# An encoder layer's routing stage: where the low one-hots are made, where the first expert rows stand, and how early the gate's weights are split

## The chip, the cores and the metric

The kernel runs on one core of a Trainium2 chip. The metric is the device time of one execution in microseconds; three runs of the kernel before are shown, and their median counts. The engines are TensorE (PE, with its weight loads PEld), VectorE (DVE), ScalarE (ACT), GpSimd (POOL) and SyncE (SP). SyncE issues most transfers, GpSimd the gathers, ScalarE some stores.

## What is computed

One encoder layer on 512 tokens of width 1024 in float32: attention, a layer norm, then a feed-forward part that picks experts per token (PEER), plus a gated embedding, and a second layer norm. The change touches the part behind the attention:

```python
q = (xb @ w_q).reshape(PEER_CHUNK, PEER_HEADS, PEER_KEY_DIM)
s1 = jnp.einsum('thd,kd->thk', q[..., :half], sub_keys[0])
s2 = jnp.einsum('thd,kd->thk', q[..., half:], sub_keys[1])
v1, i1 = lax.top_k(s1, PEER_TOPK)
v2, i2 = lax.top_k(s2, PEER_TOPK)
...
idx = (e1 * PEER_N_KEYS + e2).reshape(PEER_CHUNK, PEER_HEADS * PEER_TOPK)
g = jax.nn.softmax(cv.astype(jnp.float32), axis=-1).reshape(PEER_CHUNK, -1).astype(xb.dtype)
u = u_table[idx]
hpre = jnp.einsum('td,ted->te', xb, u)
act = g * jax.nn.gelu(hpre, approximate=False)
return jnp.einsum('te,ted->td', act, v_table[idx])
...
gate = jax.nn.sigmoid(h @ ple_gate_w[i] + ple_gate_b[i])
h = layer_norm(DN_ALPHA * h + ffn + ple, ln2_g[i], ln2_b[i])
```

## The kernel before

The 512 tokens are four chunks of 128. Every token has 128 picks among 16384 experts. Three ways of using the expert tables stand side by side. For chunk 0 the picked rows of both tables are gathered, one row per token at a time (128x1024, 512 KB). Chunk 1, called own in the code, gathers its rows of the first table (`rows`, L960 to L968: a gather by GpSimd, then a multiply and sum on VectorE) and uses the second table densely. Chunks 2 and 3 use both tables densely: TensorE multiplies all 128 blocks of 128 experts with the tokens, and a dense matrix of weights, mostly zero, picks out what counts.

**The dense weights** are made by `build_g` (L885), once each for chunks 2, 3 and 1, in 16 steps of eight tokens (OT). A step makes one-hots `oh` of the two halves of each expert's number on VectorE (L934), multiplies the first half's one-hots with the weight, once with its high part in 16 bits and once with the rest (`ow_hi`, `ow_lo`, L945, both on VectorE), and has TensorE multiply the one-hots (32 matmuls of 128x128, L912, `products`). ScalarE copies the sums out (`g_st`, L923, `leave`) and every second step sends 1 MB to DRAM (L926).

**Splits.** TensorE's operands in 32 bits are split into a high and a low part, and three matmuls (`mm3`, L111 to L113) make one product. ScalarE makes the high part, VectorE the rest. The gate's weights go through `gate_cut` (L1054): `g_hi` on ScalarE, `g_lo` on VectorE (L1059).

**The order of the work** is the order in which the code issues it, on all engines. Two parts run interleaved. The main line works on VectorE: the last searches of the query projection (a loop over g of 2 to 16, one projection of 24 matmuls a step, and the search for the 16 best keys on VectorE), `route` for the half of chunk 1, the searches that were put off (`later`), `route` and `build_g` for chunks 2 and 3, the searches and `route` of chunk 0, and the last `build_g`. Behind each piece, `run` (L1138) lays in work of the second line, `pe_work` (`gate_and_leads`, L1094), for as many microseconds as the piece yielded, times PACE; AHEAD is a lead of 14. That line has eight blocks of the first table (FIRST; eight matmuls a block, L1030, tiles `raw` or, for the first EARLY of them, `early`), then 16 steps of the gate with a block behind each (three behind a half), then blocks up to 104 (LEAD). `run` also lays in rows of chunk 1, `own`, by a share of the same amounts (OWN, OWN_SOON, OWN_G). In the projection loop `own` gets a fixed amount per step (OWN_B: 3.6 in steps 9 to 11, 2.3 from 12 on) and one more row behind the search from step 12 on. A row there has the tile `row` with two buffers; later the names `whi`, `wlo`, `row` take turns, six buffers in all.

Small pieces of the second line (the split of the gate's next weights, and `gate_end`, which adds the bias, applies tanh on ScalarE and multiplies with the tile `pl`, L1071 to L1082) wait in a list `tasks`, of which one is issued at every second matmul of a block. A load on SyncE's queue that must wait holds all loads that were issued behind it.

## Time and profile before

| | us |
|---|---|
| median of three runs | 1570.45 (1569.98 to 1571.4) |
| the profiled execution, its own time | 1569.65 |
| its span, first to last instruction | 1567.9 |
| TensorE busy | 1473.4 |
| VectorE busy | 1280.0 |
| ScalarE busy | 542.1 |
| GpSimd busy | 613.4 |

The engine columns are busy time within the span. A row of the time line has the start, the duration, the engine, the line of the kernel, the operation, the tiles written and read, and in brackets how long the engine had stood idle and what ended that. PEclk is the part of TensorE's full clock that was granted. One float32 matmul of a block shows as two records. The mean rate of the transfers over the span is 291 GB/s; between 573.8 and 782.5 us it is 392 to 397 GB/s.

### The profile page before, as it was taken

Reading aid. Unit: us, or ns where it says so; the run is one execution under the profiler, and the core shown is the slowest. Engines: PE = TensorE matmul, PEld = TensorE weight load, DVE = VectorE, ACT = ScalarE, POOL = GpSimd, SP = SyncE. Lnnn points to the kernel's source line nnn. Section 1 sums busy time; section 2 is a strip of 40 time slices with the busy share of each in tenths; the row PEclk is TensorE's granted clock in tenths of the full one; section 3 lists DMA queues with packets and bytes.
Section 4 is the critical chain, followed back from the end, with each engine's and each line's share of the span. In section 5 each row is a group of like instructions: output and inputs, shape, how many; then the busy total and the mean of one; then the engine's idle time right before and its main releaser. Section 6 shows DMA issues by size and latency. Waiting matters only on the chain.

```text
span 1567.9 us, 21888 instructions
## 1 busy us (share of the span) xinstructions
PE 1473.4 (94%) x7715; PEld 1231.0 (79%) x7715; DVE 1280.0 (82%) x2636; ACT 542.1 (35%) x915; POOL 613.4 (39%) x534
## 2 busy tenths in 40 slices
PE   6999999999878999989999889999899999999996
PEld 4788777788767877777787778888788888888885
DVE  7366795657679999899998967988788998899998
ACT  3265784433211132212322223443333333333332
POOL 1013110043443344445205526667434456545650
PEclk9999999999989999999999999999999999999998
DMA  7233340334678899999979999999999999999992
GB/s 231 64 112 92 89 128 28 93 126 136 227 252 278 311 337 374 418 403 397 384 228 364 415 405 379 403 398 392 381 398 392 367 398 385 392 392 391 368 327 91
DMA packets 189856, 460.36 MB, mean 294 GB/s; under 512 B 16561, under 2 KB 80433, under 8 KB 186673
## 3 DMA queue, kind: packets, MB, share of 16 engines
q1 hardware_dynamic: 121552, 213.55, 38.4%
q0 software_dynamic: 58400, 208.69, 35.6%
q10 hardware_dynamic: 9792, 36.70, 5.8%
q8 instruction: 61, 1.00, 0.3%
q14 instruction: 51, 0.41, 0.1%
HBM read 415.11 MB, written 40.89 MB: 291 GB/s over the span
## 4 chain that ended last, share of the span: by engine, by line
PE 56%; DVE 15%; issue 11%; POOL 8%; DMA 8%; ACT 1%; POOLq 0%; SPq 0%; DVEq 0%; ACTq 0%
PE acc L111 10%; PE acc L113 10%; PE acc L112 10%; DMA row<-in_u_rows_dram,s_ix 4%; PE pj L111 3%; PE pj L112 3%; PE pj L113 3%; POOL row L965 3%; POOL wlo L965 3%; POOL whi L965 3%; PE mm L111 2%; PE mm L113 2%; PE mm L112 2%; DMA raw<-in_uT_dram 1%; PE hp L1030 1%
## 5 line engine op out<-in xcount | busy, mean ns | idle before, releaser
L1030 PE MATMUL mm<-whole,raw 128*128 128x256 f32 x1168 | 270.0, 387 | 8.6 <-DMA raw<-in_uT_dram 8.6
L1295 POOL DMA_INDIRECT gat<-in_v_rows_dram,i_sel x128 | 191.4, 1495 | 167.0 <-DVE base L1297 134.9
L1030 PEld LDWEIGHTS mm<-whole,raw 128*128 128x128 f32 x1168 | 221.3, 193 | 41.1 <-DMA raw<-in_uT_dram 5.6
L111 PE MATMUL acc<-v_hi,a_hi 128*128 128x512 f32 x456 | 179.1, 393 | 4.0 <-ACT v_hi L96 4.0
L112 PE MATMUL acc<-v_lo,a_hi 128*128 128x512 f32 x456 | 178.8, 392 | 0.5 <-DVE v_lo L97 0.5
L113 PE MATMUL acc<-v_hi,a_lo 128*128 128x512 f32 x456 | 178.4, 391 | 0.1
L1280 POOL DMA_INDIRECT gat<-in_u_rows_dram,i_sel x89 | 134.0, 1505 | 110.4 <-DVE gat L1286 75.6
L1297 DVE SCALAR_TENSOR_TENSOR base<-gat,hdot,base 128x1024 f32<-128x1024 f32 x128 | 165.1, 1290 | 1.6
L97 DVE TENSOR_TENSOR wlo<-raw,whi 128x1024 fp32r<-128x1024 f32 (+4 forms) x103 | 118.8, 1153 | 47.4 <-ACT whi L96 45.3
L96 ACT CAST v_hi<-v_raw 128x1024 fp32r<-128x1024 f32 x76 | 79.8, 1053 | 180.5 <-issue 101.5
L96 ACT CAST whi<-raw 128x1024 fp32r<-128x1024 f32 (+4 forms) x103 | 102.5, 995 | 90.6 <-PE pj L112 22.2
L111 PE MATMUL acc<-whi,a_hi 128*128 128x512 f32 x312 | 123.0, 396 | 0.7 <-ACT whi L96 0.7
L113 PE MATMUL acc<-whi,a_lo 128*128 128x512 f32 x312 | 123.4, 396 | 0.0
L112 PE MATMUL acc<-wlo,a_hi 128*128 128x512 f32 x312 | 123.3, 396 | 0.0
L97 DVE TENSOR_TENSOR v_lo<-v_raw,v_hi 128x1024 fp32r<-128x1024 f32 x76 | 92.5, 1218 | 22.0 <-ACT v_hi L96 22.0
L1286 DVE SCALAR_TENSOR_TENSOR gat<-gat,h 128x1024 f32<-128x1024 f32 x89 | 105.0, 1220 | 0.0
L111 PEld LDWEIGHTS acc<-v_hi,a_hi 128*128 128x128 f32 x456 | 86.1, 189 | 22.5 <-ACT v_hi L96 4.4
L113 PEld LDWEIGHTS acc<-v_hi,a_lo 128*128 128x128 f32 x456 | 86.0, 189 | 19.2 <-DVE a_lo L97 0.6
L112 PEld LDWEIGHTS acc<-v_lo,a_hi 128*128 128x128 f32 x456 | 86.2, 189 | 18.5 <-DVE v_lo L97 1.0
L965 POOL DMA_INDIRECT row<-in_u_rows_dram,s_ix x52 | 63.0, 1212 | 83.5 <-DVE row L967 53.4
L967 DVE SCALAR_TENSOR_TENSOR row<-row,h_s 128x1024 f32<-128x1024 f32 x52 | 67.6, 1301 | 26.8 <-DMA row<-in_u_rows_dram,s_ix 26.8
L1030 PE MATMUL hp<-whole,raw 128*128 128x256 f32 x368 | 84.6, 385 | 0.4 <-ACT ge L1014 0.4
(394 smaller groups left out, 3328.9 us busy)
## 6 DMA issues: line engine op xcount, KB each, us to landing
raw<-in_uT_dram SPq DMA_DIRECT2D x120, 512.0 KB
v_raw<-in_v_rows_dram SPq DMA_DIRECT2D x78, 512.0 KB
raw<-in_v_rows_dram SPq DMA_DIRECT2D x50, 512.0 KB
g_dram<-g_st ACTq DMA_DIRECT2D x24, 1024.0 KB
ge_dram<-ge ACTq DMA_DIRECT2D x44, 256.0 KB
g_wide<-g_dram SPq DMA_DIRECT2D x9, 1024.0 KB
raw<-in_w_in_dram SPq DMA_DIRECT2D x17, 512.0 KB
raw<-in_w_q_dram SPq DMA_DIRECT2D x16, 512.0 KB
```

Source lines behind the costliest of these rows:

```text
L96: nc.scalar.copy(hi, src)
L97: nc.vector.tensor_tensor(lo, src, r32(hi), op=OP.subtract)
L111: nc.tensor.matmul(ps, a[0], b[0], start=start, stop=False)
L112: nc.tensor.matmul(ps, a[0], b[1], start=False, stop=False)
L113: nc.tensor.matmul(ps, a[1], b[0], start=False, stop=stop)
L965: nc.gpsimd.indirect_dma_start(out=u[:], out_offset=None, in_=u_rows, in_offset=bass.IndirectOffsetOnAxis(ap=ix[:, k:k + 1], axis=0))
L967: nc.vector.scalar_tensor_tensor(u, u, 1.0, x, op0=OP.mult, op1=OP.mult, accum_out=dots[:, k:k + 1])
L1030: nc.tensor.matmul(ps[:, :N_U], raw[:, k], whole[:, k, :], start=(k == 0), stop=(k == 7))
L1280: nc.gpsimd.indirect_dma_start(out=u[:], out_offset=None, in_=u_rows, in_offset=bass.IndirectOffsetOnAxis(ap=i_sel[:, c, k:k + 1], axis=0))
L1286: nc.vector.scalar_tensor_tensor(u, u, 1.0, h[c], op0=OP.mult, op1=OP.mult, accum_out=hdot[:, c, k:k + 1])
L1295: nc.gpsimd.indirect_dma_start(out=u[:], out_offset=None, in_=v_rows, in_offset=bass.IndirectOffsetOnAxis(ap=i_sel[:, c, k:k + 1], axis=0))
L1297: nc.vector.scalar_tensor_tensor(base[c], u, hdot[:, c, k:k + 1], base[c], op0=OP.mult, op1=OP.add)
```

## The change

It has three parts, and numbers that go with them.

The low one-hots: `w_lo` stays in 32 bits, one value per token and pick, and `ow_lo` is made by ScalarE, eight multiplies of 128x128 a step with the weight as a scale from the tile, instead of one VectorE instruction of 128x1024. They stand behind the copies of the sums of the step before. The yields of a step go from 2.45 to 1.8 in all.

The rows in the projection: one row before the search and one behind it, from step 12 on, instead of two and one; the row (or piece of routing) behind the search begins at step 10.

The gate's weights: `g_hi` and `g_lo` have two buffers, and the weights of step j+2 are split behind step j's matmuls, where those of step j+1 were. `pl` has three buffers instead of four and EARLY is 6 instead of 7. PACE is 1.06, OWN_G 1.5.

```diff
-PACE = 1.0
+PACE = 1.06
-EARLY = 7
+EARLY = 6
-OWN_B = (3.6, 2.3)
+OWN_B = (3.6, 1.1)
-OWN_G = 1.15
+OWN_G = 1.5
...
-        wx = [bt.tile([128, 128, 2], F16, name=n) for n in ("w_hi", "w_lo")]
-        w_ps = ps[:, 256:384].unsqueeze(2).to_broadcast([128, 128, 2])
+        w_hi = bt.tile([128, 128, 2], F16, name="w_hi")
+        w_lo = bt.tile([128, 128], F32, name="w_lo")
...
             yield 1.15
-            ow = []
-            for n, x in zip(("ow_hi", "ow_lo"), wx):
-                y = bt.tile([128, OT, 128], F16, name=n)
-                nc.vector.tensor_tensor(y.rearrange("p t (a b) -> p t a b", b=2),
-                                        oh[:, 0].rearrange("p t (a b) -> p t a b", b=2),
-                                        x[:, t0:t0 + OT].unsqueeze(2).to_broadcast([128, OT, 64, 2]), op=OP.mult)
-                ow.append(y)
-                if n == "ow_hi":
-                    yield 0.65
+            ow = [bt.tile([128, OT, 128], F16, name=n) for n in ("ow_hi", "ow_lo")]
+            nc.vector.tensor_tensor(ow[0].rearrange("p t (a b) -> p t a b", b=2),
+                                    oh[:, 0].rearrange("p t (a b) -> p t a b", b=2),
+                                    w_hi[:, t0:t0 + OT].unsqueeze(2).to_broadcast([128, OT, 64, 2]), op=OP.mult)
             if ahead:
                 leave(ahead[0], sums)
+            for t in range(OT):
+                nc.scalar.mul(ow[1][:, t], oh[:, 0, t], w_lo[:, t0 + t:t0 + t + 1])
...
-        hi = rw.tile([128, 512], F32R, name="g_hi")
-        lo = rw.tile([128, 512], F32R, name="g_lo")
+        hi = rw.tile([128, 512], F32R, name="g_hi", bufs=2)
+        lo = rw.tile([128, 512], F32R, name="g_lo", bufs=2)
...
-            pl[c] = rg.tile([128, 512], F32, name="pl", bufs=4)
+            pl[c] = rg.tile([128, 512], F32, name="pl", bufs=3)
...
+        def cut_next():
+            w, cut = gate_cut(graw.pop(0))
+            ws.append(w)
+            return [cut[0], nothing, cut[1]]
+
         for n in range(FIRST):
-            if n == FIRST - 2:
-                w, cut = gate_cut(graw.pop(0))
-                tasks.extend([cut[0], nothing, cut[1]])
+            if n >= FIRST - 2:
+                tasks.extend(cut_next())
             yield from lead_block()
+        graw += [gate_raw(2), gate_raw(3)]
...
-            if j + 1 < 16:
-                w, cut = gate_cut(graw.pop(0))
-                if j + 2 < 16:
-                    graw.append(gate_raw(j + 2))
-                tasks[0:0] = [cut[0], nothing, cut[1]]
+            if j + 2 < 16:
+                tasks[0:0] = cut_next()
+                if j + 4 < 16:
+                    graw.append(gate_raw(j + 4))
...
-            if g > 11:
+            if g > 9:
                 next(own)
```

Three places show how the order of the instructions changes. The first is VectorE in the projection loop, steps 13 and 14; `row` is a gathered row of chunk 1, `sc` the scores that are searched. Before:

```order
L692 MAX_INDEX i_all<-v_all,tk_t 128x8
L967 SCALAR_TENSOR_TENSOR row,s_dot<-row,h_s 128x1024 x3
L684 MAX v_all<-sc 128x8
L686 MAX_INDEX i_all<-v_all,sc 128x8
L688 MATCH_REPLACE tk_t<-v_all,sc 128x128
L690 MAX v_all<-tk_t 128x8
```

And now:

```order
L692 MAX_INDEX i_all<-v_all,tk_t 128x8
L964 SCALAR_TENSOR_TENSOR row,s_dot<-row,h_s 128x1024 x2
L684 MAX v_all<-sc 128x8
L686 MAX_INDEX i_all<-v_all,sc 128x8
L688 MATCH_REPLACE tk_t<-v_all,sc 128x128
L690 MAX v_all<-tk_t 128x8
```

Between two searches there are two rows where there were three: the one behind the first search and one before the second.

The second place is ScalarE in the first build; `g_st` are the sums that are copied out, `ge` a block's result, `ge_dram` and `g_dram` are stores. Before:

```order
L923 ACTIVATE g_st<-tr 128x128x4 x2
L926 DMA g_dram<-g_st 128x2048
L1014 ACTIVATE ge<-mm 128x256
L923 ACTIVATE g_st<-tr 128x128x4 x2
L1014 ACTIVATE ge<-mm 128x256
L1016 DMA ge_dram<-ge 128x512
```

And now:

```order
L923 ACTIVATE g_st<-tr 128x128x4 x2
L926 DMA g_dram<-g_st 128x2048
L949 ACTIVATE ow_lo<-oh,w_lo 128x128 x8
L923 ACTIVATE g_st<-tr 128x128x4 x2
L949 ACTIVATE ow_lo<-oh,w_lo 128x128 x8
L1011 ACTIVATE ge<-mm 128x256
L923 ACTIVATE g_st<-tr 128x128x4 x2
```

Behind every pair of copies stand the eight multiplies of the next step, and they come before the following block's result.

The third place is SyncE's queue at the end of the gate's first half, with the semaphores that each load waits for; `pl` is what the gate is multiplied with, `raw` a block of the first table, `g_raw` the gate's weights. Before:

```order
L1071 DMA pl<-ple_dram 128x512 [waits DMAHW7_49]
L1071 DMA pl<-ple_dram 128x512 [waits DMAHW0_49]
L1071 DMA pl<-ple_dram 128x512
L1071 DMA pl<-ple_dram 128x512 [waits DMAHW2_49]
L1007 DMA raw<-in_uT_dram 128x1024 [waits DMAHW3_49,PE_49]
```

And now:

```order
L1048 DMA g_raw<-in_gate_w_dram 128x512 [waits DMAHW3_49,DMAHW0_49,DVE_49]
L1068 DMA pl<-ple_dram 128x512
L1068 DMA pl<-ple_dram 128x512 [waits DMAHW2_49]
L1068 DMA pl<-ple_dram 128x512
L1068 DMA pl<-ple_dram 128x512 [waits DMAHW5_49,DMAHW1_49,DVE_49]
L1004 DMA raw<-in_uT_dram 128x1024 [waits DMAHW6_49,PE_49]
```

The fourth load of `pl` now waits for VectorE, and the loads of `raw` stand behind it.

More of the change, by code (lines that the diff above doesn't have):

```diff
@@ L898, in build_g @@
                            .unsqueeze(3).to_broadcast([128, nq, OT, 2]))
-        wx = [bt.tile([128, 128, 2], F16, name=n) for n in ("w_hi", "w_lo")]
-        w_ps = ps[:, 256:384].unsqueeze(2).to_broadcast([128, 128, 2])
+        w_hi = bt.tile([128, 128, 2], F16, name="w_hi")
+        w_lo = bt.tile([128, 128], F32, name="w_lo")
         scale = W_OWN if c == NGC else W_MAX
-        nc.scalar.mul(wx[0], w_ps, scale)
-        nc.vector.scalar_tensor_tensor(wx[1], w_ps, scale, wx[0], op0=OP.mult, op1=OP.subtract)
+        nc.scalar.mul(w_hi, ps[:, 256:384].unsqueeze(2).to_broadcast([128, 128, 2]), scale)
+        nc.vector.scalar_tensor_tensor(w_lo, ps[:, 256:384], scale, w_hi[:, :, 0], op0=OP.mult, op1=OP.subtract)
         yield 0.5
@@ L1096, in gate_and_leads @@
         graw = [gate_raw(0), gate_raw(1)]
+        ws = []
+        def cut_next():
+            w, cut = gate_cut(graw.pop(0))
+            ws.append(w)
+            return [cut[0], nothing, cut[1]]
         for n in range(FIRST):
-            if n == FIRST - 2:
-                w, cut = gate_cut(graw.pop(0))
-                tasks.extend([cut[0], nothing, cut[1]])
+            if n >= FIRST - 2:
+                tasks.extend(cut_next())
             yield from lead_block()
+        graw += [gate_raw(2), gate_raw(3)]
         for j in range(16):
@@ L1107, in gate_and_leads @@
             k = j % 8
+            w = ws.pop(0)
             for c in range(4):
```

## The prediction

> **What bounds the kernel now.** I read the page first, for which engine is full, then the waits of TensorE, then the time line at those waits, and last a table by stage.
>
> ```profile
> PE 1473.4 (94%) x7715; PEld 1231.0 (79%) x7715; DVE 1280.0 (82%) x2636; ACT 542.1 (35%) x915; POOL 613.4 (39%) x534
> PE   6999999999878999989999889999899999999996
> ```
>
> TensorE is busy for 94% of the span, and the change leaves its work alone. So a gain can only come out of the 94.5 us in which it is idle and out of its slow clock. The slices put most of the idle time between 400 and 960 us: the end of the query projection, the gate and the routing. All edits lie there. After that TensorE is full, and a gain made before is kept.
>
> The waits of TensorE from 380 to 500 us, the column being total, times and longest, and the time line of TensorE there:
>
> ```profile
> PE mm L112 <- DVE g_lo L1059: 14.2, 2, 10.2
> PE mm L113 <- POOL wlo L768: 5.2, 2, 2.8
> 400.00:420.00 20.00, 14.81 (x65) 11.67 (x65) 14.29 (x27) 3.50 (x10) 9.46 (x7) 0.91 0.63 197
> 402.39 0.40 PE L111 MATMUL mm<-hTh,whi 128*128 128x512 f32 x1
> 402.63 0.40 PE L112 MATMUL mm<-hTl,whi 128*128 128x512 f32 x1
> 425.87 1.05 PE L727 MATMUL tr<-skT,q_t 128*128 128x128 f32 x8
> 426.76 20.94 PE L1030 MATMUL hp<-whole,early 128*128 128x256 f32 x96
> 450.80 0.58 PE L111 MATMUL mm<-g_hi,hTh 128*128 128x512 f32 x1
> 461.56 0.80 PE L112 MATMUL mm<-g_lo,hTh 128*128 128x512 f32 x1 [10.18 <-DVE g_lo L1059]
> 462.15 0.63 PE L113 MATMUL mm<-g_hi,hTl 128*128 128x512 f32 x1
> 462.58 0.63 PE L111 MATMUL mm<-g_hi,hTh 128*128 128x512 f32 x1
> 474.37 0.80 PE L112 MATMUL mm<-g_lo,hTh 128*128 128x512 f32 x1 [4.07 <-DVE g_lo L1059]
> ```
>
> TensorE stands for 5.2 us in the projection and for 14.2 us at the first two gate steps. Behind the gate waits the clock is low: the matmuls start 0.43 us apart (462.15 to 462.58) where they started 0.24 us apart before (402.39 to 402.63). Why the split of the gate's weights came so late, the time line of VectorE shows:
>
> ```profile
> 414.28 3.08 DVE L967 SCALAR_TENSOR_TENSOR row<-row,h_s 128x1024 f32<-128x1024 f32 x1 [1.59 <-DMA row<-in_u_rows_dram,s_ix]
> 445.10 0.29 DVE L684 MAX8 v_all<-sc 128x8 f32<-128x128 f32 x1
> 460.82 0.69 DVE L1059 TENSOR_TENSOR g_lo<-g_raw,g_hi 128x512 fp32r<-128x512 f32 x1
> ```
>
> TensorE computed the scores of the last but one projection at 425.87, and VectorE began the last search at 445.10, some 19 us behind. Each step gives VectorE three rows of 512 KB with two buffers to gather into, so it waits for transfers. The split at 460.82 follows only after the routing that stands before it.
>
> The table by stage has a row from each one-hot build or routing to the next (busy us of PE, PEld, DVE, ACT and POOL, granted clock, DMA share, GB/s):
>
> ```profile
> 448.00:471.30 23.30, 12.12 (x44) 9.50 (x42) 20.82 (x82) 2.83 (x5) 10.20 (x9) 0.78 0.82 285
> 471.30:513.50 42.20, 39.13 (x163) 32.87 (x164) 38.17 (x161) 5.41 (x12) 15.31 (x12) 0.92 0.85 279
> 513.50:573.80 60.30, 58.15 (x260) 48.29 (x259) 57.43 (x158) 13.95 (x28) 25.23 (x20) 1.00 0.89 314
> 573.80:665.50 91.70, 83.67 (x560) 72.11 (x559) 82.29 (x123) 26.20 (x54) 42.13 (x32) 0.98 1.00 392
> 665.50:714.20 48.70, 43.57 (x200) 37.22 (x200) 45.76 (x140) 8.80 (x19) 22.46 (x19) 1.00 1.01 397
> 714.20:782.50 68.30, 63.67 (x452) 54.11 (x452) 63.96 (x96) 20.65 (x43) 25.90 (x20) 0.98 0.99 396
> 782.50:831.80 49.30, 49.24 (x242) 43.27 (x241) 44.78 (x238) 10.56 (x24) 3.56 (x4) 1.00 0.74 229
> 831.80:929.90 98.10, 85.08 (x545) 72.20 (x544) 84.07 (x127) 23.63 (x50) 47.13 (x37) 0.95 1.02 411
> ```
>
> The builds (rows four, six, eight) have a DMA share of about 1 at 392 to 411 GB/s, and neither TensorE nor VectorE is full in rows four and eight: transfers end last there. Row seven is the opposite, TensorE full and transfers at 229.
>
> **The projection and the gate.** In after, steps 12 to 16 do one row before the search and one after it. Eleven rows instead of 15 are done when the searches end. Two buffers then serve two rows, and the wait for GpSimd's split goes, since that split stood in GpSimd's queue behind gathers which waited for VectorE. Worth: the 5.2 us, and 20 x (1 - 0.91) = 1.8 us of clock: 7 us. VectorE then follows TensorE by one search and two rows, some 6 us, not 19. TensorE still has seven blocks to do before the first gate step (426.76 to 450.80, 24 us), so the split is there in time even without the second pair of tiles. That removes 14.2 us, and 24 matmuls x 0.19 us = 4.6 us of clock: 19 us. If VectorE were still late, the 19 would come back; that is a rival.
>
> How far this shortens the way to the first one-hot (573.80) is counted along TensorE's order. After 425.87, now 418.9, the order has 192 block matmuls before that point in after (184 before) and 64 gate steps (58). A block matmul is two of the records of the row at 426.76, 20.94 / 48 = 0.43 us with the last one's tail left out; a gate step is three matmuls, 0.70 us with its gaps as an estimate from the 0.24 spacing. So 192 x 0.43 + 64 x 0.70 = 127.5, which ends at 546.4. VectorE has about 116.4 us (20.82 + 38.17 + 57.43) from 424.5 on, or 541, with room for 5 us of waits.
>
> **A new wait in SyncE's queue.** The tile pl now has three buffers for four loads. The fourth load waits until VectorE has used the first, and SyncE holds all later loads of raw behind it.
>
> ```profile
> 512.87 2.29 SPq L1071 DMA_DIRECT2D pl<-ple_dram  x4
> 515.26 0.39 SPq L1007 DMA_DIRECT2D raw<-in_uT_dram  x1
> 517.17 3.18 PE L1030 MATMUL hp<-whole,raw 128*128 128x256 f32 x14
> 524.65 3.69 PE L1030 MATMUL hp<-whole,raw 128*128 128x256 f32 x16 [0.41 <-ACT ge L1014]
> 525.64 0.69 DVE L1081 SCALAR_TENSOR_TENSOR mm<-mm,pl 128x512 f32<-128x512 f32 x1
> 442.63 4.20 DMA row<-in_u_rows_dram,s_ix
> ```
>
> The raw issued at 515.26 is for the block that starts at 524.65, the third after the gate's half. In after it goes out only after the instruction that in before runs at 525.64, so at about 526.5. With 4.2 us of landing (the gather of equal size at 442.63) it is there at 531, 6 us after 524.65. Bounds: 0, if VectorE gets there earlier, and 9 with a longer landing and a slow clock. I take 7, on the path, at the first half: 546.4 becomes 553.4, that is 20.4 before 573.8. The second half's wait falls into the first build, where transfers end last; it costs 0 there, or 7 if that cover is gone.
>
> **The low one-hots on ScalarE.** Durations by form, of VectorE and of ScalarE, and from ScalarE's time line two copies that follow each other and the issue of a transfer:
>
> ```profile
> L945 DVE TENSOR_TENSOR ow_lo<-oh,w_lo 128x1024 f16<-128x1024 f16 x48 | 32.8, 684 | 0.0
> L923 ACT ACTIVATE g_st<-tr 128x512 f32<-128x512 f32 x96 | 52.5, 595 | 79.7 <-PE tr L912 70.6 <-issue 8.2 <-ACT ge L1014 0.8
> L1014 ACT ACTIVATE ge<-mm 128x256 f32<-128x256 f32 x65 | 25.0, 384 | 153.9 <-PE mm L1030 148.2 <-remote 4.6 <-ACT g_st L923 0.8
> L99 ACT ACTIVATE cqh<-pj,gq 128x512 fp32r<-128x512 f32 x3 | 2.0, 680 | 0.0
> L279 ACT COPY v_na<-pj 128x512 f32<-128x512 f32 x4 | 2.4, 588 | 15.8 <-PE pj L113 15.8
> L980 ACT ACTIVATE s_dot<-s_dot 128x128 f32<-128x128 f32 x1 | 0.3, 310 | 2.6 <-DVE wlo L967 2.6
> 387.06 0.38 ACT L738 COPY back<-tr 128x256 f32<-128x256 f32 x1
> 387.32 0.28 ACT L739 COPY geb<-tr 128x128 f32<-128x128 f32 x1
> 600.85 0.33 ACTq L926 DMA_DIRECT2D g_dram<-g_st  x1
> ```
>
> 48 multiplies of 0.684 us leave VectorE, 32.8 us. ScalarE gets 48 x 8 of 128x128 with a scale from a tile. No row shows that form. An instruction of that size takes 0.31 us (s_dot); a scale from a tile adds 0.09 (cqh against v_na); one behind another starts 0.12 us before the first ends (387.06 to 387.32). Bounds are 0.19 and 0.40 us each; I take 0.31 + 0.09 - 0.10 = 0.30, 2.4 us for the eight. The Trainium skill (ScalarE: Activation LUTs, Rules for kernel authors) says to multiply on VectorE rather than ScalarE. The trace agrees on the work, 2.4 against 0.684 us; whether it costs time is the third rival. ScalarE was busy for 26.2 of 91.7 us in the first build.
>
> The yields per step of a build are smaller by 0.65, and PACE is 1.06, so fewer rows and blocks are laid into the builds. Counted in the order, before against after: first build 34 rows and 149 block matmuls against 25 and 117; second 26 and 119 against 25 and 101; third 38 and 154 against 38 and 137; searches and routing before the third build none and 106 against 14 and 153.
>
> Each section, from its row in the table:
> - First build: it moved 91.7 x 0.392 = 35.9 MB. Nine rows and four raws less (0.524 MB each) and some spill are 28.6 MB, at 411 GB/s 70 us. TensorE 83.67 - 32 x 0.43 - 6 x 0.70 = 66; ScalarE 26.2 + 38.4 = 65. I take 72: -20.
> - Routing behind it: five more block matmuls, TensorE 46: -3.
> - Second build: TensorE 56, transfers (27.0 - 2.4 MB) 60, ScalarE 59 and its waits for TensorE. I take 64: -4.
> - Searches and routing: TensorE 49.24 + 47 x 0.43 = 69: +20.
> - Third build: transfers (40.3 - 1.3 MB) 95: -3.
>
> Together -10 us. Six fewer block matmuls in all are done by then; they follow later, +2.6.
>
> **The sum**, against the profiled execution's own 1569.65 us (1.75 over its span, 0.8 under the median): -20.4 - 10 + 2.6 = -28, so 1541.8, and some 1542 beside the median of 1570.45.
>
> **The rivals.** Second, the load of pl hides (-7) and the first two builds end with their transfers, at 70 and 60 (-6): 1529. For it: the wait is worked out from where VectorE stood in before. Against it: that instruction waits for the gate's own matmuls, not for VectorE's lead.
>
> Third, slower: ScalarE paces the builds. One step of it is two g_st (1.1 us), 0.9 of a ge (0.35), issues (0.3: half a g_dram of 0.33 and as much of a spill), 0.5 as an estimate for TensorE's answer, and eight multiplies: 2.25 + 8m. The three builds after are 231 us, 4.8 a step; the 28 us are gone at 4.8 + 28 / 48 = 5.4, where m = 0.39. At 0.45 it is 5.85 x 48 = 281, so 1542 + 50 = 1592. For it: without overlap m is 0.40. By the rule of the Trainium skill named above it would be this one. Against it: ScalarE's instructions overlap in the rows above.
>
> Fourth, the gate is not cured: VectorE is still late, or a load behind the new order is, and the 19 us stay: 1561. For it: the second split now needs its raw tile earlier. Against it: 24 us of blocks stand before it.
>
> **The numbers.** Forecast 0.60, second 0.18, fourth 0.12, third 0.07, rest 0.03. A measurement of this kernel tells about 0.2%, 3 us, from no change. The forecast and the second are faster, and the fourth too: 0.88 with part of the rest; 0.04 within 0.2%; slower 0.08. The range reaches from under the second to the fourth: 1526 to 1563.
>
> **What would show it.** Right: no wait of TensorE for g_lo over 1 us before 480; the first one-hot near 553; the eight multiplies at 2.2 to 2.6 us; a wait of TensorE for raw of about 6 us soon after the gate's first half; transfers at over 390 GB/s in the first and third build. Wrong: TensorE waiting for ow_lo at every step of a build (third rival), or the first one-hot after 565 (fourth).

## The result, and the profile after

The changed kernel takes 1577.59 us (median of 12 runs, 1574.57 to 1585.48) beside 1569.61 us (median of 12) for the kernel before. The ratio is 1.0053, with a 95% interval of 1.0035 to 1.007: slower by half a per cent. The forecast was 1542. The profiled execution is the uppermost of the 12 (1585.48 us, span 1583.6), so its stages add up to some 8 us more than the median does.

The page of the changed kernel, first the busy times and TensorE's slices:

```profile
PE 1487.7 (94%) x7715; PEld 1237.0 (78%) x7715; DVE 1246.8 (79%) x2588; ACT 652.4 (41%) x1299; POOL 622.7 (39%) x534
PE   6999999999987989999898879999899999999996
```

TensorE's work is the same 7715 instructions, and VectorE has lost the 33 us of the low one-hots. The weak slices of TensorE still stand in the same stretch. The waits of TensorE there, from 380 to 500 us and, behind the dots, from 500 to 600:

```profile
PE hp L1027 <- DMA raw<-in_uT_dram: 4.1, 2, 2.2
PE mm L113 <- POOL wlo L768: 1.7, 2, 1.0
PE mm L112 <- DVE g_lo L1056: 0.9, 1, 0.9
...
PE hp L1027 <- DMA raw<-in_uT_dram: 16.2, 2, 8.5
```

The kernel before had one wait for `raw` from 380 to 600 us:

```profile
PE mm L1030 <- DMA raw<-in_uT_dram: 0.4, 1, 0.4
```

The wait for `g_lo` has gone from 14.2 to 0.9 us and that for `wlo` from 5.2 to 1.7, as forecast. But 20.3 us of waits for `raw` have taken their place. TensorE's time line shows where they are:

```profile
420.49 1.05 PE L727 MATMUL tr<-skT,q_t 128*128 128x128 f32 x8
464.03 3.69 PE L1027 MATMUL hp<-whole,raw 128*128 128x256 f32 x16 [1.88 <-DMA raw<-in_uT_dram]
472.69 5.38 PE L1027 MATMUL hp<-whole,raw 128*128 128x256 f32 x16 [2.17 <-DMA raw<-in_uT_dram]
515.01 5.46 PE L1027 MATMUL hp<-whole,raw 128*128 128x256 f32 x12 [8.49 <-DMA raw<-in_uT_dram]
582.97 6.67 PE L1027 MATMUL hp<-whole,raw 128*128 128x256 f32 x16 [7.67 <-DMA raw<-in_uT_dram]
```

Two small waits stand in the first half of the gate and a large one behind each half. SyncE's queue shows why; a row here is a group of loads with its first issue and the time from there to its last. First some of its waits from 436 to 600 us, then its time line at the two halves:

```profile
SPq L1048 <- DVE g_lo L1056: 55.4, 11, 6.7
...
SPq L1068 <- DMA pl<-ple_dram: 12.3, 2, 8.1
...
SPq L1068 <- DVE mm L1078: 6.5, 1, 6.5
```

```profile
501.40 6.87 SPq L1068 DMA_DIRECT2D pl<-ple_dram  x4
508.70 1.63 SPq L1004 DMA_DIRECT2D raw<-in_uT_dram  x3
559.43 16.40 SPq L1068 DMA_DIRECT2D pl<-ple_dram  x4
575.94 1.99 SPq L1004 DMA_DIRECT2D raw<-in_uT_dram  x3
```

In the kernel before, the loads of `pl` behind the second half took 3.06 us (2.29 behind the first, as shown with the prediction):

```profile
568.78 3.06 SPq L1071 DMA_DIRECT2D pl<-ple_dram  x4
```

VectorE's instructions that free the first buffer of `pl`:

```profile
507.23 0.70 DVE L1078 SCALAR_TENSOR_TENSOR mm<-mm,pl 128x512 f32<-128x512 f32 x1 [0.65 <-DMA pl<-ple_dram]
573.67 1.21 DVE L934 TENSOR_TENSOR oh<-iota,ex 128x2048 f16<-128x2048 f16 x1
574.80 0.68 DVE L1078 SCALAR_TENSOR_TENSOR mm<-mm,pl 128x512 f32<-128x512 f32 x1
```

Four loads of `pl` take SyncE 6.87 and 16.40 us, because the fourth stands until VectorE has done L1078 (507.23 and 574.80). In the first half VectorE is not what is late: it stood for the first `pl` itself (the 0.65 us in its row), which took from 501.40 to about 507.1 to land. In the second half the landing of a `pl` holds SyncE for 8.1 us, and VectorE for 6.5 us more. Three `raw` go out together right behind, at 508.70 and 575.94, and TensorE has run dry by then.

The line with `g_lo` for L1048 is the load of the gate's weights: now four steps ahead, it is issued ahead of the split that frees its buffer, and SyncE stands there 11 times. It stood there as often in the kernel before, and longer:

```profile
SPq L1051 <- DVE g_lo L1059: 96.4, 11, 41.0
```

But there the load stood behind the split that it waited for, and TensorE waited 0.4 us for a `raw` in all. What is new is the place of the load in the queue, not the wait; run 6 below tries it.

The first one-hot (573.67) is where it was before (574.16): all that was won at the projection and the gate is gone there. The table by stage continues from it, with the columns of the table of before: first build, routing, second build, searches and routing, third build, and what follows to the start of stage 2.

```profile
573.70:649.50 75.80, 67.31 (x443) 54.74 (x442) 59.13 (x85) 54.87 (x164) 29.19 (x23) 0.93 0.91 347
649.50:702.10 52.60, 49.56 (x231) 41.83 (x230) 46.01 (x139) 12.67 (x31) 22.04 (x19) 0.97 1.02 401
702.10:766.00 63.90, 59.28 (x425) 48.72 (x424) 54.14 (x78) 55.84 (x167) 30.97 (x24) 1.00 1.02 408
766.00:838.60 72.60, 69.66 (x334) 60.44 (x334) 60.76 (x265) 13.43 (x32) 15.06 (x16) 1.00 0.83 299
838.60:931.00 92.40, 78.45 (x499) 66.46 (x498) 73.05 (x110) 57.28 (x167) 49.44 (x35) 0.91 1.00 397
931.00:960.00 29.00, 22.20 (x104) 18.70 (x103) 6.93 (x11) 7.43 (x19) 12.73 (x11) 0.88 1.01 383
```

The first build moves 347 GB/s, where it moved 392 before. The loss is in the us behind the late `raw`; below are ten of them, with GpSimd's wait (from 570 to 600 us) and VectorE's (from 576 to 600):

```profile
583.70:593.70 10.00, 10.00 (x47) 8.29 (x46) 3.45 (x5) 3.62 (x11) 0.94 (x1) 0.74 0.48 143
POOL row L962 <- DVE row L964: 12.4, 1, 12.4
DVE oh L934 <- PE tr L912: 6.8, 2, 6.5
```

The late tile holds TensorE, VectorE waits for TensorE's products, and the next gather waits for VectorE. So the transfers of this stage do not end last: for a while they are not issued.

The second build is near the forecast (63.9 for 64). The row of the third ends where VectorE's last work for it does; ScalarE's multiplies, a wait for `raw` (3.26 us) and the products follow. From its `w_lo` to its last product it takes 100.0 us and took 99.6 before, so it is not shorter. The last row is the second surprise: TensorE is busy for 22.20 of 29 us at a clock of 0.88.

The new instructions on ScalarE, the group and then two steps of its time line:

```profile
L949 ACT ACTIVATE ow_lo<-oh,w_lo 128x128 f16<-128x128 f16 x384 | 117.2, 390 | 14.2 <-ACT g_st L923 6.5 <-DVE oh L934 6.5 <-issue 0.4
```

```profile
601.13 2.44 ACT L949 ACTIVATE ow_lo<-oh,w_lo 128x128 f16<-128x128 f16 x8
603.47 0.37 ACT L1011 ACTIVATE ge<-mm 128x256 f32<-128x256 f32 x1
```

One multiply takes 0.390 us by itself, but eight take 2.34 us from the first's start to the next instruction's (601.13 to 603.47): 0.29 each, forecast 0.30. The Trainium skill (ScalarE: Activation LUTs, What ACT_TABLE_LOAD costs) gives 186 ns, 93 for the scale from a tile and 0.833 an element, which makes an estimate of 386 ns here, and an overlap of 93: the trace agrees with both (390 and about 100).

### The profile page after: what moved, and what is told of

It is laid out like the page before. It is cut to its first block, busy times and chain, and to the rows that moved or that the text cites. A ratio compares the mean times of both kernels' runs of the same rounds, so it can differ in the third digit from the quotient of the medians.

```text
span 1583.6 us, 22228 instructions
## 1 busy us (share of the span) xinstructions
PE 1487.7 (94%) x7715; PEld 1237.0 (78%) x7715; DVE 1246.8 (79%) x2588; ACT 652.4 (41%) x1299; POOL 622.7 (39%) x534
## 4 chain that ended last, share of the span: by engine, by line
PE 56%; issue 12%; DVE 12%; DMA 11%; POOL 7%; ACT 2%; SPq 0%; POOLq 0%; ACTq 0%; DVEq 0%
PE acc L111 10%; PE acc L113 10%; PE acc L112 10%; PE pj L111 3%; PE pj L112 3%; PE pj L113 3%; POOL row L962 3%; DMA raw<-in_uT_dram 3%; POOL whi L962 2%; PE mm L111 2%; DMA row<-in_u_rows_dram,s_ix 2%; PE mm L113 2%; POOL wlo L962 2%; PE mm L112 2%; DMA whi<-in_u_rows_dram,s_ix 2%
## 5 line engine op out<-in xcount | busy, mean ns | idle before, releaser
L111 PE MATMUL acc<-v_hi,a_hi 128*128 128x512 f32 x456 | 179.4, 394 | 5.9 <-ACT v_hi L96 5.9
L1284 POOL DMA_INDIRECT gat<-in_u_rows_dram,i_sel x89 | 140.6, 1580 | 101.0 <-DVE gat L1290 75.9
L111 PE MATMUL acc<-whi,a_hi 128*128 128x512 f32 x312 | 123.0, 396 | 0.5 <-ACT whi L96 0.5
L949 ACT ACTIVATE ow_lo<-oh,w_lo 128x128 f16<-128x128 f16 x384 | 117.2, 390 | 14.2 <-ACT g_st L923 6.5
L1027 PE MATMUL hp<-whole,raw 128*128 128x256 f32 x384 | 95.9, 408 | 23.8 <-DMA raw<-in_uT_dram 23.8
L1027 PEld LDWEIGHTS hp<-whole,raw 128*128 128x128 f32 x384 | 78.7, 206 | 38.6 <-issue 16.9
L111 PEld LDWEIGHTS acc<-v_hi,a_hi 128*128 128x128 f32 x456 | 86.2, 189 | 24.5 <-ACT v_hi L96 6.3
```

Source lines behind the costliest of these rows:

```text
L111: nc.tensor.matmul(ps, a[0], b[0], start=start, stop=False)
L949: nc.scalar.mul(ow[1][:, t], oh[:, 0, t], w_lo[:, t0 + t:t0 + t + 1])
L1027: nc.tensor.matmul(ps[:, :N_U], raw[:, k], whole[:, k, :], start=(k == 0), stop=(k == 7))
L1284: nc.gpsimd.indirect_dma_start(out=u[:], out_offset=None, in_=u_rows, in_offset=bass.IndirectOffsetOnAxis(ap=i_sel[:, c, k:k + 1], axis=0))
```

## The experiments

Each run was timed beside the kernel before on the same chip (medians 1569.88, 1570.48, 1570.52 and 1570.74 us in the four groups of four). Theory Q says that SyncE's queue gives the gain back, S that ScalarE paces the builds, T that transfers from the first one-hot to stage 2 absorb what is gained earlier, L that blocks left behind the last build do it. The times, and five places of each profiled execution as far as the text uses them (first one-hot; start of the third build, its `w_lo`; last one-hot product on TensorE; first product of stage 2, L111; span), in us. The places are those of one execution, which lies up to 8 us from its run's median:

| run | median | ratio to before (95%) | first one-hot | third build | last product | stage 2 | span |
|---|---|---|---|---|---|---|---|
| before | 1569.6 | | 574.2 | 831.8 | 931.4 | 943.0 | 1567.9 |
| after | 1577.6 | 1.0053 (1.0035-1.007) | 573.7 | 838.6 | 938.6 | 958.4 | 1583.6 |
| 1 projection alone | 1564.5 | 0.9973 (0.996-0.9986) | 559.0 | 826.4 | 922.6 | 931.3 | 1561.4 |
| 2 projection and gate | 1575.0 | 1.0039 (1.0023-1.0056) | 564.0 | 839.8 | 937.2 | 943.6 | 1575.5 |
| 3 builds alone | 1576.8 | 1.0049 (1.0031-1.0066) | 579.3 | 833.0 | 920.4 | 952.0 | 1576.5 |
| 4 after, pl free | 1565.8 | 0.9973 (0.9958-0.9987) | 568.0 | 823.0 | 918.0 | 939.9 | 1564.8 |
| 5 run 2, pl free | 1566.3 | 0.9985 (0.9968-1.0002) | | | | | 1559.5 |
| 6 after, pl and g_raw free | 1560.1 | 0.9933 (0.9911-0.9954) | 560.3 | 819.3 | 913.8 | 935.5 | 1560.3 |
| 7 run 4, PACE 1.12 | 1575.9 | 1.0026 (1.0008-1.0044) | 580.7 | 843.9 | 944.0 | 925.0 | 1578.6 |
| 8 run 4, more on ScalarE | 1584.1 | 1.008 (1.0054-1.0106) | 570.1 | 843.7 | 936.5 | 957.5 | 1580.8 |
| 9 after, pl free in second half | 1570.6 | 0.9993 (0.9975-1.0011) | | | | | 1572.4 |
| 10 run 6, builds on VectorE | 1561.9 | 0.9938 (0.9915-0.9961) | 557.1 | 823.7 | 919.7 | 925.3 | 1561.1 |
| 11 run 6, PACE 1.0 | 1574.4 | 1.002 (1.0004-1.0036) | 557.4 | 806.6 | 904.7 | 951.1 | 1573.7 |
| 12 run 6, six on ScalarE | 1558.7 | 0.9923 (0.9901-0.9945) | | | | | 1559.1 |
| 13 run 6, PACE 1.24 in third build | 1557.1 | 0.9923 (0.9904-0.9942) | 559.7 | 817.3 | 909.6 | 917.5 | 1553.0 |
| 14 before, pl in three buffers | 1586.8 | 1.0113 (1.0091-1.0136) | 581.2 | 848.8 | 947.7 | 960.2 | 1585.2 |
| 15 after, g_raw free | 1574.5 | 1.0025 (1.001-1.0041) | | | | | 1573.0 |
| 16 run 6, six, PACE 1.18 in third | 1555.6 | 0.9907 (0.9888-0.9926) | 563.6 | 821.1 | 914.1 | 924.7 | 1552.6 |

### The parts by themselves

Run 1, on the kernel before:

```diff
-OWN_B = (3.6, 2.3)
+OWN_B = (3.6, 1.1)
...
-            if g > 11:
+            if g > 9:
```

> The kernel before with one part of the change alone: steps 10 to 16 of the projection do one row of the own gather after the search (g > 9 instead of g > 11) and OWN_B is (3.6, 1.1); gate, pl, EARLY and builds as before. Three theories are weighed over these four runs. Q (SyncE's queue): the parts gain what was forecast, and SyncE's queue, held by loads that wait for VectorE, gives it back. S (ScalarE): the 0.39 us multiplies pace the builds, and the loss is made there. T (transfers): from the first one-hot to the start of stage 2 the gathers and loads are the bound, so what is gained earlier is waited for later. Before is 1570. By Q: the g_lo wait of 14.2 us and most of the wlo wait of 5.2 us go, with no new wait of SyncE, so the time is 1570 - 19 = 1551, at most 1558. By S: the same as Q, 1551 to 1558, since the builds are untouched. By T: the first one-hot moves from 574 to about 555, and the time moves by no more than a third of that, 1564 to 1570.

It gained 5.4 us. The first one-hot came 15 us earlier, but of the wait for `g_lo`, 16.4 us from 380 to 600 us in the kernel before, more than half remained. The waits of TensorE from 380 to 600 us in this run:

```profile
PE mm L112 <- DVE g_lo L1059: 9.0, 4, 6.3
PE mm L113 <- POOL wlo L768: 1.9, 3, 1.0
```

The rows alone do bring the first split nearly in time: TensorE waits 0.52 us for it, where it waited 10.18. The second split is still late (6.29 us, 4.07 before); the second pair of tiles cures it (0.7 us in all in run 2). Of the 15 us two thirds are lost behind the first one-hot, as T expected.

Run 2 is the changed kernel without its builds (`ow_lo`, `w_lo`, PACE and OWN_G as before); run 3 the kernel before with them alone. The core of run 2's edit on the changed kernel; run 3 has its reverse on the kernel before:

```diff
-PACE = 1.06
+PACE = 1.0
-OWN_G = 1.5
+OWN_G = 1.15
...
-            for t in range(OT):
-                nc.scalar.mul(ow[1][:, t], oh[:, 0, t], w_lo[:, t0 + t:t0 + t + 1])
```

> The changed kernel with its builds put back: both weighted one-hots on VectorE, PACE 1.0, OWN_G 1.15; it keeps the rows on either side of the search, the gate split two steps ahead in two tiles, pl in three buffers and EARLY 6. By Q: waits for raw of about 8 us behind each half of the gate as in the changed kernel, the first one-hot near 574, and the time within 5 us of before, 1565 to 1575, so some 15 to 20 above the run with the projection part alone. By S: the time is under the changed kernel's 1577 by all that the builds lose, 1555 to 1566. By T: 1568 to 1574, whatever the first one-hot does.

> The kernel before with the low weighted one-hots on ScalarE alone, with PACE 1.06 and OWN_G 1.5 of the changed kernel; projection, gate, pl in four buffers and EARLY 7 as before. By Q: the builds gain the 7 us that were forecast for them, 1560 to 1567. By S: slower, 1576 to 1590, with TensorE waiting for ow_lo in most steps of a build. By T: 1568 to 1575, since gathers and loads set where the builds end with either engine.

Run 2 came out at the top of Q's range and 1 us over T's, 10.5 us slower than run 1 though it has the better gate: 20.5 us of waits for `raw`. Its first one-hot is at 564.0 and not near 574, as Q had it, since the second large wait (9.02 us) comes only behind it. Run 3 went S's way in time (+7), but not in kind: TensorE waits for ScalarE's `ow_lo` for 1.6 us in all from 560 to 960 us. The first one-hot is 5 us late there, and 31.6 us lie between the last product and stage 2 (11.6 before).

### SyncE's queue

Run 4, on the changed kernel; the two places named hold nothing that is needed any more when the load is issued:

```diff
         def load(c):
-            pl[c] = rg.tile([128, 512], F32, name="pl", bufs=3)
+            if c < 3:
+                pl[c] = rg.tile([128, 512], F32, name="pl", bufs=3)
+            elif hs.start == 0:
+                pl[c] = early_u[0][:, 0:4].rearrange("p k n -> p (k n)")
+            else:
+                pl[c] = rw.tile([128, 512], F32, name="g_raw", bufs=2)
```

> The changed kernel with the fourth load of pl given memory that is free at that time (in the first half the tile of the first early block, in the second half a g_raw tile), so that SyncE does not wait for VectorE there. The changed kernel is at 1577. By Q: the waits for raw of 8.5 and 7.7 us go with their slow clock, the first one-hot moves from 574 to about 556, and the time falls by 13 to 20 us, to 1557 to 1564. By S: it falls as far before the builds, and the builds keep their 8 us, so 1560 to 1567: this run does not part Q from S, the one with the builds alone does. By T: the waits go and the first one-hot comes earlier, and the time falls by at most 6, 1571 to 1577.

It won 11.8 us. That is less than Q's range and inside that of S, and the first one-hot came 5.7 us earlier where Q had 18; so the wait is real, but priced too high by Q. T is out for this wait. Run 5 is the same on run 2:

> The changed kernel with the fourth pl load in free memory (as in the fourth run) and its builds put back to VectorE (as in the second run). After four runs the waits of SyncE (Q) stand with some 12 us between the changed kernel and the fourth run, and the builds cost 7 alone. For these 7 there are two theories. S (ScalarE): the multiplies of 0.39 us pace the builds. L (leftover blocks): the builds get shorter, but fewer block matmuls are laid into them, and those left behind the last product (23 by the order, 16 before) wait for raw tiles that land slowly, since stage 2's gathers have begun. Q expects 1575 - 12 = 1563 here, 1559 to 1567. T, that transfers make the early gain worthless, expects 1570 or more. Against the fourth run's 1566, S and L both expect 2 to 6 less.

8.8 us came back (runs from 1561 to 1576, so a rough number). S and L had both expected run 5 to be 2 to 6 us faster than run 4. With the two equal, the builds cost nothing once `pl` is free. Run 6 also issues the load of the gate's weights behind the split:

```diff
-                tasks[0:0] = cut_next()
+                cut = cut_next()
                 if j + 4 < 16:
-                    graw.append(gate_raw(j + 4))
+                    split = cut.pop()
+                    cut.append(lambda j=j, split=split: (split(), graw.append(gate_raw(j + 4))))
+                tasks[0:0] = cut
```

> The fourth run's kernel, and the load of g_raw(j+4) issued behind the split of j+2, no longer ahead of it, so that the raw of the block that follows is not queued behind a load that waits for VectorE. In the fourth run TensorE waits 2.15 us (464) and 5.24 us (509) for raw. Q, in full: both waits go, with about 2 us of slow clock, and the time falls by 5 to 9 to 1557 to 1561. If the 5.24 us is the landing of a burst (four pl and three raw issued within 6 us), it stays, only the 2.15 goes, and the time is 1563 to 1567.

5.7 us more. Of the 20.3 us of waits for `raw` this is left, in TensorE's waits of run 6 from 430 to 600 us:

```profile
PE hp L1027 <- DMA raw<-in_uT_dram: 3.9, 2, 3.1
```

Without these waits the change is 17.5 us faster than it was made, and 0.7% faster than the kernel before. Run 9 frees `pl` in the second half only (`if c < 3 or hs.start == 0`), run 15 only the load of `g_raw`, and run 14 gives the kernel before `pl` in three buffers (`bufs=4` to `bufs=3`) and nothing else:

> The changed kernel with the fourth pl load in free memory in the gate's second half only; in the first half it waits for VectorE as in the changed kernel. This parts the 12 us between the changed kernel and the fourth run by halves. By the prediction, in which the second half's wait is hidden by the first build's transfers, nothing comes of it: 1575 to 1578. By Q with the traces of the changed kernel (the first build and the routing behind it took 128.6 us there and 118.4 in the fourth run, the first one-hot was 5.7 later), the second half is the larger: 6 to 10 less, 1567 to 1572.

> The changed kernel with the load of g_raw(j+4) behind the split of j+2, and pl still held as in the changed kernel. If the two waits of SyncE add up, this gives the 5.7 us between the fourth and the sixth run: 1571 to 1573. If pl's wait covers what g_raw's gives back, since the blocks stand for the same raw tiles anyway, less than 2: 1576 to 1578.

> The kernel before with pl in three buffers for four, and nothing else. It prices the wait of SyncE alone, where VectorE is as late as in the kernel before. By Q the price is that of the pair of changed kernels, 12 us, or more since VectorE is further behind TensorE here: 1580 to 1588. By the prediction it is 7: 1575 to 1578. By T it is mostly absorbed by what ends last later: 1570 to 1574.

The second half is worth 7.0 us (1577.6 to 1570.6) and the first 4.8 (to 1565.8), but the 4.8 is not clear of the noise: the intervals of runs 9 and 4 overlap. `g_raw` alone gives 3.1 and not the 5.7 that it gives once `pl` is free. That would fit if the wait for `pl` covers part of the other, since TensorE stands for the same tiles; but 3.1 is not clear of the noise either. In the kernel before, one buffer less costs 16.1 us. VectorE is later there: SyncE stands for it at these loads for 19.1 us (L1071 behind L1081), 6.5 in the changed kernel. SyncE's time line in run 14 shows the same picture, with longer waits than in the changed kernel:

```profile
510.80 13.81 SPq L1071 DMA_DIRECT2D pl<-ple_dram  x4
524.73 1.57 SPq L1007 DMA_DIRECT2D raw<-in_uT_dram  x3
...
575.78 19.25 SPq L1071 DMA_DIRECT2D pl<-ple_dram  x4
595.15 1.87 SPq L1007 DMA_DIRECT2D raw<-in_uT_dram  x3
```

The Trainium skill (DMA: Bandwidth & Descriptors, Rules for kernel authors) advises to issue a transfer early and wait for it late. Run 6 beside run 4 goes the other way for a load whose buffer is still in use: issued later, behind the split, it gained 5.7 us.

### ScalarE and the builds

Run 8 adds work to ScalarE (first edit, on run 4), run 12 moves some of it to VectorE (second edit, on run 6), and run 10 puts the builds of run 6 back to VectorE:

```diff
+            more = bt.tile([128, 128], F16, name="more", bufs=1)
+            for t in range(2):
+                nc.scalar.mul(more, oh[:, 0, t], w_lo[:, t0 + t:t0 + t + 1])
```

```diff
+            for t in range(2):
+                nc.vector.tensor_scalar(ow[1][:, t], oh[:, 0, t], w_lo[:, t0 + t:t0 + t + 1], None, op0=OP.mult)
-            for t in range(OT):
+            for t in range(2, OT):
                 nc.scalar.mul(ow[1][:, t], oh[:, 0, t], w_lo[:, t0 + t:t0 + t + 1])
```

> The fourth run's kernel with two more multiplies of 128x128 on ScalarE in each of the 48 steps of the builds, into a tile that nothing reads: 48 x 2 x 0.39 = 37 us more of ScalarE. S: if ScalarE paces the builds, all of it shows, 1590 to 1603. L: ScalarE has slack in each step, and the time stays within 4 us of 1566, 1562 to 1570.

> The sixth run's kernel with two of the eight low multiplies of each step on VectorE, one 128x128 instruction each. The reverse of the eighth run, in which 37 us more of ScalarE by durations (28 by spacing, 0.29 us each) cost 18. By S (ScalarE sets the step) 28 us of ScalarE go and the time falls by up to 18 less VectorE's part (96 instructions of about 0.15 us, 14): 1546 to 1558. If ScalarE stands level with the other engines and only becomes the bound with more work, the time stays or VectorE's 14 us show in part: 1558 to 1568.

> The sixth run's kernel (neither pl nor g_raw holds SyncE) with its builds put back: both weighted one-hots on VectorE, PACE 1.0, OWN_G 1.15. Against the sixth run it gives what the low one-hots on ScalarE are worth when nothing else is late. The prediction had them at -7: 1567 here. By the pair of the fourth and the fifth run (1565.8 and 1566.3) they are worth nothing: 1558 to 1563. By the run with the builds alone (+7) they cost: 1553 to 1556.

28 us more on ScalarE (96 x 0.29) cost 18.2, between what S and L expected. 28 less gained 1.5, inside the intervals; but VectorE got 96 multiplies of 0.25 us for them (24 us, expected 14), so this run does not show what less work on ScalarE alone is worth. It fits that ScalarE stands level with the other engines: more of it shows, and moving it does not help. The first build of run 6 says so too, with TensorE at 64.42 of 66 us and ScalarE at 54.66 besides its issues:

```profile
559.00:625.00 66.00, 64.42 (x437) 52.78 (x436) 56.52 (x81) 54.66 (x163) 28.59 (x22) 1.00 0.99 387
```

Run 10 is at 1561.9 and run 6 at 1560.1: the low one-hots on ScalarE are worth 1.7 us, which is inside the noise. S is out as the cause of the loss.

### What follows the third build

Runs 7, 11, 13 and 16 move block matmuls of the second line about, by PACE (1.12 in run 7, 1.0 in run 11) or, in runs 13 and 16, by a larger PACE in the third build only (below for run 13; 1.18 in run 16):

```diff
-        due += amount * PACE
+        due += amount * pace
...
         own_due = 0.0
+        pace = 1.24
         run(build, OWN_G)
```

> The fourth run's kernel with PACE 1.12 for 1.06: more block matmuls are laid beside VectorE's work, and none is left behind the last product by the order (23 in the fourth run). L: the stretch from the last product to stage 2 falls from 21.9 us to under 10; of these 12 us the 10 us of work that the 23 matmuls are come back in the earlier stages where TensorE is full, so the time falls by 2 to 8, to 1558 to 1564. S: nothing is won, since ScalarE's step is as long as before and TensorE's answers to it come later: 1566 to 1575.

> The sixth run's kernel with PACE 1.0 for 1.06: fewer block matmuls are laid beside VectorE's work (192 for 200 ahead of the first build, 745 for 801 by the last product) and 55 instead of 23 are left behind the last product. If the first builds end with TensorE (busy for 64.4 of 66 us in the sixth run), the first one-hot and the first builds come some 5 us earlier each; by L the 32 more matmuls behind the last product cost 14 us of work and, at transfers of some 11 us a tile, up to 20. Sum: 1560 to 1572, slower than the sixth run's 1560. If TensorE's share does not matter, 1558 to 1562.

> The sixth run's kernel with PACE 1.24 in the third build alone, 1.06 up to there as before: its spare TensorE time (79 us busy of 95) takes the 23 block matmuls that were left behind the last product, and none is left by the order. L (leftover blocks): the stretch from the last product to stage 2 falls from 21.7 us to 8 or less, with the 4.9 us wait for raw in it, and the third build gets no longer, so the time falls by 6 to 12, to 1548 to 1554. T (transfers): the third build and the tail both move data at a share of 1.02; the three raw tiles are loaded earlier but push the rows back, the build gets longer by what the tail gets shorter, and the time stays within 3 us of 1560, 1557 to 1563.

> Neither pl nor g_raw holds SyncE, six of eight low multiplies on ScalarE and two on VectorE (as in the twelfth run), and PACE 1.18 in the third build alone, with 10 block matmuls left behind its last product. By L: 1558.7 less half of what the thirteenth run gains, 1551 to 1556. By T: 1556 to 1562.

The counts in these expectations leave out the blocks whose tile is `whi` or `wlo`. With them, 24 block matmuls stand behind the last product in the kernel before, 31 in the changed one and runs 4 and 6, 42 in run 3, 87 in run 11, 13 in runs 1, 2 and 10, 10 in run 16 and none in runs 7 and 13. From the last product to stage 2 it is 11.6, 19.8, 21.9 and 21.7, 31.6, 46.4, 8.7, 6.4 and 5.5, 10.6 and (run 13) 7.9 us. From 13 on, the more are left, the longer; with fewer it does not follow the count. This is what such a stretch looks like, on TensorE in run 6, from the last product to stage 2:

```profile
913.83 0.31 PE L912 MATMUL tr<-ow_lo,oh 128*128 128x128 f16 x1
913.94 4.73 PE L1027 MATMUL mm<-whole,raw 128*128 128x256 f32 x14
918.51 3.62 PE L1027 MATMUL hp<-whole,raw 128*128 128x256 f32 x16
926.98 5.41 PE L1027 MATMUL hp<-whole,raw 128*128 128x256 f32 x16 [4.85 <-DMA raw<-in_uT_dram]
932.22 3.62 PE L1027 MATMUL hp<-whole,whi 128*128 128x256 f32 x16
935.49 0.47 PE L111 MATMUL hp<-hTh,whi 128*128 128x256 f32 x1
```

31 x 0.43 is 13 of the 21.7 us; the rest is the wait for `raw` (4.85) and a slow clock (0.85 from 914 to 935.5). The loads land late, among the gathers of stage 2 that have begun; from 905 to 945 us in run 4 a `raw` of 512 KB lands 11.0 us after its issue (the last number of the row):

```profile
raw<-in_uT_dram SPq DMA_DIRECT2D x6, 512.0 KB, 11.0
```

Yet L is only half right. Run 11, with the most left, is 14.3 us slower than run 6, as L had it and 2 us over its range. But run 7, with none left, is 10.1 us slower than run 4 and outside the ranges of both theories: with the blocks laid in earlier the first one-hot is 12.7 us later than in run 4 and the third build 20.8 us later, and stage 2 begins before the last product. Run 13 takes the blocks into the third build, which gets no longer (817.3 to 909.6, 92.3 us, beside 94.6), and stage 2 starts 18.0 us earlier, but the median falls by 3.0 only, which is in T's range and not clear of the noise. TensorE's waits from 905 to 942 us in run 13 tell where the 18 us went:

```profile
PE acc L111 <- ACT a_hi L96: 8.0, 1, 8.0
PE hp L111 <- ACT whi L96: 7.6, 1, 7.6
PE hp L111 <- ACT ge L1012: 4.3, 1, 4.3
```

Stage 2 now waits 19.9 us for its own first tiles, where it waits 1.2 us in run 6; two of these three are splits whose own wait was for transfers (`whi` on a `raw` of stage 2 for 8.1 us, `a_hi` on `g_near`, the dense weights read back from DRAM, for 7.9). With less left behind the build, the tiles of stage 2 are late next. Run 16 adds the small gains of runs 12 and 13 up to 1555.6 us, 0.9% under the kernel before, the best of all.

## Why the prediction was wrong, step by step

**The projection: right, a little large.** The scores of the last but one projection came at 420.49 us for 425.87, 5.4 us earlier; the forecast had 7.

**The gate: right in effect, wrong in one reason.** The wait for `g_lo` fell from 14.2 to 0.9 us. That the split is in time "even without the second pair of tiles" was right for the first split (10.18 to 0.52 us in run 1) and wrong for the second (6.29 us left).

**A new wait in SyncE's queue: this step failed.** The mechanism was named: the fourth load of `pl` holds the loads of `raw` behind it. For the first half the price was not far off (7, measured 4.8), though there it was the landing of the first `pl` and not VectorE's place that set it. "It costs 0 there" for the second half was wrong: 7.0 us by run 9. The cover was that transfers end last in the first build. But the late `raw` holds TensorE, then VectorE and the gathers, and so the issue of those very transfers: it is no cover, and the first build fell to 347 GB/s. First build and routing took 129.2 us (572.87 to 702.08) in the changed kernel and 119.2 in run 6; the forecast was 72 + 46 = 118. And the load of `g_raw`, which the same edit moved ahead of the split that frees its buffer, was not priced at all: 5.7 us by run 6. These waits together cost 17.5 us for 7, and without them the change is a gain. The fourth rival came nearest, a load behind the new order that is late in place of the gate's split; it too was too fast, at 1561.

**The way to the first one-hot: its count stopped too early.** In the kernel before, the count of TensorE's work ends at the transposes of the indices, and it was compared with the place behind them. Its time lines of TensorE and of VectorE:

```profile
569.62 0.38 PE L891 MATMUL tr<-ident,e 128*128 128x128 f32 x2
```

```profile
573.82 0.43 DVE L903 SCALAR_TENSOR_TENSOR w_lo<-tr,w_hi 128x256 f16<-128x256 f32 x1 [1.38 <-ACT w_hi L902]
```

That is 4.2 us. `w_lo` came at 572.87 us, 19.5 behind the forecast's 553.4. Of these, 4.2 are this slip, 1.6 the projection, and 6.4 SyncE's waits up to there (13.4 between the changed kernel and run 6, 7 foreseen). Of the other 7.3, run 6 still has 3.1 us in a wait for `raw`; the last 4.2 stay open.

**The low one-hots: price right, sum too good.** 0.29 us each for 0.30, and the third rival's condition (0.39) was not met. In place of -7.4 for the builds and the blocks behind them, -4.0 with the eight block matmuls (3.4 us) that PACE lays ahead of the first build, it was -1.7, which is not clear of the noise. By stage, run 6 beside run 10: 3.2 us later at the first one-hot, -20.8 to the second build (forecast -23), +13.2 to the third (+16), -1.4 to the last product (-3), and +5.1 from there to the end, where the forecast had 2.6 for six block matmuls (seven by the traces). The left-over blocks are that last term (31 here, 13 in run 10, 24 in the kernel before): 16.1 us more from the last product to stage 2, and 11.0 less behind its start. Priced by their work alone, they also wait for their tiles.

**The sum for the profiled execution.** 1585.48 against 1541.8 is 43.7: 19.5 to the first one-hot, 11.2 in the first build and routing, 3.5 in the second build, searches and routing (136.5 for 133), 9.0 from the third build to stage 2 (119.7 for 95 + 2.6 and the 13.1 from 929.9 to 943.0 in the kernel before), and 0.5 behind it. SyncE's queue explains the sign, but not the whole of it. By the medians the forecast missed by 36 us, and 10.5 of them are these waits beyond the 7 foreseen. The other 25 are in run 6 too. Without the 7, its profiled execution is over the forecast by 13.1 us up to the first `w_lo`, 1.2 in the first build and routing, 7.6 from there to the third build and 5.5 from there to stage 2.

**"A gain made before is kept": not in every run.** From the start of stage 2 to the end of the span it is 624.9 us in the kernel before, 625.2 in the changed one and 624.8 in run 6, as the prediction had it. But it is 630.1 in run 1, 631.9 in run 2, 635.8 in run 10 and 635.5 in run 13, where fewer blocks are left ahead of it (13, 13, 13 and none): a part of the gain is lost behind that start.

**What stays open.** Even without SyncE's waits a gain ahead of the first one-hot came through by half: run 10 has it 17.1 us earlier than before and ends 8.6 us earlier by the median, run 1 15.1 and 5.4. In run 10 the start of stage 2 is 17.8 us earlier too, and 10.9 us are lost behind it; run 13 shows stage 2's first tiles as one place where that happens. That the four rows moved out of the projection, with the block matmuls laid beside them, make the stretch before the third build longer (127.2 us in run 10 from the second one-hot build to the third `w_lo`, 117.3 before) fits the order but was not tried by itself. Nor was EARLY, 6 for 7, or the first half's `pl` alone.

## What to carry to other kernels

A load that waits for a buffer in an in-order queue cost in these runs what stood behind it, not what it carries; before taking a buffer away, look up when its reader runs, when the first load lands, and which loads are queued behind. That a stage's transfers end last was no cover for a wait which, through the engines behind it, stops the issue of those transfers. Work left over behind a stage is to be priced with the landing of its tiles among the next stage's transfers, and what is late next is to be looked for before its gain is counted.

## What had not been expected of the hardware

A `raw` of 512 KB landed in 11.0 us (median of run 4, 905 to 945 us) with the transfers at a share of 1.02, where the estimate had a gather of equal size at 4.2. And one late tile brought the transfers of a full stage down to 143 GB/s for ten us, because the gathers wait for VectorE, and VectorE waits for TensorE.
